# Middle rows of an expert transposed within the next expert's up products, gathers issued earlier in the program, combine weights of all tokens made together

## The chip, the cores and the metric

The kernel runs on one core of a Trainium2 chip. Its engines are named as the profile names them: PE (TensorE, the matrix products), DVE (VectorE), ACT (ScalarE), POOL (GpSimd) and SP (SyncE, which here only issues transfers). Each works through its own queue of instructions in the order in which the program was laid out, and waits at the head of the queue for data or for a buffer. The metric is the device time of one execution in microseconds (us); lower is better.

## The reference

One layer over 512 tokens of width 1024, in float32. Three token mixers (a gated delta rule and two linear attentions with decays) share one input projection, are gated, summed and projected; the result goes through a layer norm. Then comes the part that the change touches, a mixture of 16 experts with a hidden width of 256, of which each token uses two:

```
scores = sigmoid(t @ w_router)
... (one group of four experts is picked, then the top 2 in it: e_idx)
w_sel = take_along_axis(scores, e_idx); w_sel = w_sel / sum(w_sel)
combine = sum(one_hot(e_idx, 16) * w_sel)
h = silu(t @ w_gate[e]) * (t @ w_up[e])
y = sum over e of (h * combine[e]) @ w_down[e]
```

A last layer norm over `alpha*h + y` gives the output.

## The kernel before

The mixers fill the time up to about 635 us, layer norm and routing the time to about 690 us, the experts that to about 853 us, and the rest is the last layer norm and the stores.

A product in float32 is made of three products of rounded halves. `split` (L315) makes them: ACT copies a tile into a rounded high part (CAST, L321), DVE subtracts it from the tile to get the low part (L322). `mm3` (L333) then issues high times high, high times low, low times high (PE, L337 to L339). For weights the high and low parts live in rings of five buffers each (rr_75, 76, 77 and fr_5760, 5761 hold high parts, rr_78, 79, 80 and fr_5762, 5763 low parts), so a cast waits until PE has used the tile five before.

The rows of a token group are handled by slots: each expert has 128 slots. `slots` (L1485) builds one-hot matrices on DVE (L1496) and small products on PE (L1498, L1510) that give, per slot, the token to gather (gidx), the place to scatter to (sidx) and its combine weight (wsl). It does so for four experts at a time, in two experts of the steady part, called slot experts below. For each expert e then:

- `fetch` (L1593) issues its weight transfers on SP (`weights`, six tiles: four of gate and up, two of down), gathers its token rows xg from memory by an indirect transfer on POOL (L1526) into one of three buffers, and transposes xg in `ex_in` (L1536): eight 128x128 transposes on PE (L1541), whose result is split by ACT (L1533) and DVE (L1534) into the tiles xT.
- `ex_up` (L1545) makes the gate and up products: four units u = 0 to 3, each one split weight tile and 6 products, 24 in all.
- `ex_down` (L1560) makes the hidden row (silu on ACT L1562, times up and combine weight on DVE L1563), transposes it (two transposes on PE, L1566), splits the transposed row into the tile mh (ACT CAST L1569, DVE subtraction L1570), then makes 12 down products in two units, copies them out (ACT, L1578) and scatters them (POOL, L1579).

The loop over experts (L1635) calls `ex_up(e)`, then `ex_down(e-1)`, then `fetch(e+1)`, and hooks can insert work behind a unit of `ex_up`. This is the program's order. Each engine's queue is laid out from it by a scheduler that may move instructions of different tiles past each other, when the kernel is built. In the result each PE period holds 24 up products of one expert, two transposes of the row before, eight transposes of the row after, and 12 down products. In this document h0 to h15 are the pairs of row transposes L1566 of experts 0 to 15.

The routing (`choose`, L1315) finds the mask Mb of the chosen experts for two token tiles at a time and hands back `weigh` (L1361), eight small DVE operations (L1364 to L1371) that normalise the scores and put the combine weights, cut in three bf16 pieces, into rc. For tiles 0 and 1 they are called while the first layer norm of tiles 2 and 3 still runs, for tiles 2 and 3 in `slots23`. Instructions of this phase that are pinned to a written order are shown as line L149.

Of the kernel before, what the change touches and what calls it, by code (L numbers as in the profile page):

```python
# [20 lines left out]
T = 512  # L21
# [17 lines left out]
def kernel(  # L39
# [85 lines left out]
    def scr():  # L125
        return scrp.tile([P, T], F32, name="scr", tag="scr", bufs=4)
# [9 lines left out]
    def flat(a):  # L136
        return a.rearrange("p a b -> p (a b)")
# [1004 lines left out]
    E = 16  # L1142
# [174 lines left out]
    def choose(n0, n1, V):  # L1317
# [42 lines left out]

        def weigh():  # L1361

            w = rt[:, 5]
            V.tensor_mul(w, sc, mk)  # L1364
            V.tensor_reduce(um[:, 2], w, axis=mybir.AxisListType.X, op=ALU.add)
            V.reciprocal(um[:, 3], um[:, 2])
            V.tensor_mul(w, w, um[:, 3][:, :, None].to_broadcast([P, m, E]))
            V.tensor_copy(rc[:, n0:n1, :, 3], w)
            V.tensor_sub(w, w, rc[:, n0:n1, :, 3])
            V.tensor_copy(rc[:, n0:n1, :, 4], w)  # L1370
            V.tensor_sub(rc[:, n0:n1, :, 5], w, rc[:, n0:n1, :, 4])  # L1371
# [57 lines left out]
    for n in range(NT):  # L1429
        ps = pst(pp)  # L1430

        between = [lns[i][1](c) for i, c in (((0, 0), (1, 0)), ((0, 1), (2, 0)), ((1, 1), (3, 0)), ((2, 1),))[n] for _ in range(1)]
        steps = [g for g in between for _ in range(2)]
        for u in range(4):
            last = wo_mm(n, u, ws[u], ps)
            if u < len(steps):
                next(steps[u])
            if u == (0 if n == NT - 1 else 2) and n:
                lns[n - 1][4]()
            if u == 2 and n:  # L1440
                lns[n - 1][2]()
            if u == (0 if n == NT - 1 else 2) and n:
                lns[n - 1][3]()
            if u == 2 and n == 2:
                choose(0, 2, V)()
            if u == 2 and n == 3:
                ranks(0, 2, V)
            if u == 3 and n < 2:
                ready.append(split(first[0][n], *(new((P, 2, T), F32R, at="fr") for _ in range(2)), pinned=True))
        lns[n][0](1, ps)  # L1450
# [8 lines left out]
        pass  # L1459
    scores()  # L1460
    rows()
    weigh = choose(2, 4, W)
    ranks(2, 4, W)
    rows0(1, 1, 2)
    drop(*x4)
# [59 lines left out]
    def gather(dst, idx):  # L1525
        return nc.gpsimd.indirect_dma_start(  # L1526
            out=dst, out_offset=None, in_=h1d, in_offset=bass.IndirectOffsetOnAxis(ap=idx, axis=0),
            bounds_check=T - 1, oob_is_err=False)
# [28 lines left out]
                hook[u]()  # L1557
        return ps

    def ex_down(ps, raw, wcol, sidx_col, m=2 * T, e=0):  # L1560
        sg = scr()
        S.activation(sg[:, 0:256], ps[:, 0:256], AF.Silu)  # L1562
        V.scalar_tensor_tensor(sg[:, 256:], ps[:, 256:], wcol, sg[:, 0:256], op0=ALU.mult, op1=ALU.mult)  # L1563
        ps = pst(pm)
        for c in range(2):
            TE.transpose(ps[:, c * P:(c + 1) * P], sg[:, 256 + c * P:256 + (c + 1) * P], ident)  # L1566
        mh = scrp.tile([P, 2, 2, P], F32R, name="mh", tag="scr", bufs=4)
        hT_ = [mh[:, 0], mh[:, 1]]
        S.copy(flat(hT_[0]), ps[:, :256])  # L1569
        sub = V.tensor_sub(flat(hT_[1]), ps[:, :256], flat(hT_[0]).bitcast(F32))  # L1570
        yo = yos((P, D))
        ps = [pst(pp), pst(pp)]
        for k in range(2):
            w = split(raw[4 + k], V=G if e == E - 1 and k == 1 else V)
            for c in range(2):
                mm3(ps[c], lambda b, k: hT_[b][:, k], lambda b, k: w[b][:, c], k, k + 1, k == 0, k == 1)
        for c in range(2):
            S.copy(yo[:, c * T:(c + 1) * T], ps[c])  # L1578
        s = nc.gpsimd.indirect_dma_start(  # L1579
            out=y2d[:m], out_offset=bass.IndirectOffsetOnAxis(ap=sidx_col, axis=0), in_=yo, in_offset=None,  # L1580
            bounds_check=m - 1, oob_is_err=False)
        for o in scats:
            tc.declare_no_dep(s.ins, o.ins, reason="rows of other slots")
        scats.append(s)
        return sub
# [7 lines left out]
    def fetch(e):  # L1593
        wts = weights(e) if e > 1 else first[e]
        if e % 4 == 1 and 1 < e < E - 4:
            slots_of(e + 3, e + 7)()
        xg = xgs[e % 3]
        if e > 1:
            gather(xg, gidx[:, e:e + 1])
        return wts, ex_in(xg)  # L1600


    first.append(weights(1))
# [18 lines left out]

    def slots23():
        rest.append(slots_of(2, 4, W))
        weigh()

    def weights03():
        with tc.issue_after(lows.ins):
# [1 line left out]
        for f in rest:  # L1630
            f()

    hooks = [{2: slots23}, {1: weights03}, {1: lambda: slots_of(4, 8)()}] + [{}] * (E - 3)
    late = None
    for e in range(E):  # L1635
        if e == E - 1:
            ex_down(*late, e=e - 1)
        TE = TP if e == 0 else nc.tensor
        ps = ex_up(xT, wts, ready if e == 0 else (), e, hooks[e])
        if 0 < e < E - 1:  # L1640
            ex_down(*late)
        late = ps, wts, wsl[:, e:e + 1], sidx[:, e:e + 1]
        if e < E - 1:
            wts, xT = fetch(e + 1)
        TE = nc.tensor

    def at_end(src):
# [139 lines left out]
```

## Time and profile before

| | us |
|---|---|
| time, three runs | 887.18, 889.05, 890.28 (median 889.05) |
| the profiled execution | 887.7, its span 885.9 |
| PE busy | 825.9 (93% of the span) |
| DVE busy | 597.9 (67%) |
| ACT busy | 442.0 (50%) |
| POOL busy | 170.9 (19%) |
| mean granted clock of PE | 0.978 of full speed |

The shares are means over stages with different limits, so they don't tell what a change in the expert stage is worth; that is read from the waits and timelines of that stage. PE's records overlap one another (a product of 0.39 us is followed by the next 0.23 us after its start), so the start times tell its pace.

### The profile page before, as it was taken

To read this page: it belongs to the slowest core of one execution; us is meant where nothing else is said; L and a number is where in the kernel's file an instruction comes from. 1 tells how busy PE (TensorE), PEld (TensorE's weight loads), DVE (VectorE), ACT (ScalarE), POOL (GpSimd) and SP (SyncE) were. 2 spreads that over 40 slices of the span, in tenths; PEclk is the share of its full clock that TensorE was granted. 3 is DMA by queue.
4 is the path that set the end of the run, shared out by engine and by line. 5 is a ranking of instruction groups with operands and counts; after the bars stand their busy time and mean duration, and the time that the engine had idled before them with its cause. 6 is when DMAs were issued, how large, how long until landed. Compare 5 with 4: busy or idle time off the path is not lost. (4 is left out here: it accounts for less than half of the span.)

```text
span 885.9 us, 15191 instructions
## 1 busy us (share of the span) xinstructions
PE 825.9 (93%) x5860; PEld 693.5 (78%) x5860; DVE 597.9 (67%) x1104; ACT 442.0 (50%) x824; POOL 170.9 (19%) x197
## 2 busy tenths in 40 slices
PE   8989999999989999999999999999999899999940
PEld 5867878978887999988888888888777678777730
DVE  7775567787675655685934345445477999999838
ACT  6533456645466344475333233234223788888823
POOL 2550001440461330200000000000022132121132
PEclk9989999999999999999999999999999999999985
DMA  6512222022013221234534334336526999999143
GB/s 196 128 56 84 73 72 72 26 72 74 26 72 119 73 72 49 73 120 137 172 96 143 95 95 123 96 105 210 184 79 197 358 357 354 348 367 360 51 160 144
DMA packets 99999, 125.90 MB, mean 142 GB/s; under 512 B 12967, under 2 KB 86775, under 8 KB 99924
## 3 DMA queue, kind: packets, MB, share of 16 engines
q1 hardware_dynamic: 89344, 109.17, 38.4%
q10 hardware_dynamic: 6116, 7.48, 2.6%
q0 software_dynamic: 4464, 8.25, 2.5%
q8 instruction: 47, 0.77, 0.4%
q14 instruction: 28, 0.23, 0.1%
HBM read 118.21 MB, written 14.68 MB: 150 GB/s over the span
## 5 line engine op out<-in xcount | busy, mean ns | idle before, releaser
L322 DVE TENSOR_TENSOR rr<-ff,rr 128x1024 fp32r<-128x1024 f32 x125 | 154.6, 1244 | 112.8 <-ACT rr L321 111.5
L321 ACT CAST rr<-ff 128x1024 fp32r<-128x1024 f32 x126 | 132.1, 1053 | 164.7 <-PE ps L338 126.2
L337 PE MATMUL ps<-rh,rr 128*128 128x512 f32 x384 | 153.7, 400 | 0.0
L338 PE MATMUL ps<-rh,rr 128*128 128x512 f32 x384 | 150.8, 393 | 0.0
L339 PE MATMUL ps<-rh,rr 128*128 128x512 f32 x384 | 150.6, 392 | 0.0
L337 PE MATMUL ps<-rr,rh 128*128 128x256 f32 (+1 forms) x320 | 93.3, 292 | 0.6 <-DVE rh L149 0.6
L339 PE MATMUL ps<-rr,rh 128*128 128x256 f32 (+1 forms) x320 | 91.8, 288 | 0.9 <-issue 0.9
L338 PE MATMUL ps<-rr,rh 128*128 128x256 f32 (+1 forms) x320 | 91.3, 286 | 0.0
L337 PEld LDWEIGHTS ps<-rh,rr 128*128 128x128 f32 x384 | 72.6, 189 | 15.5 <-issue 0.8
L339 PEld LDWEIGHTS ps<-rh,rr 128*128 128x128 f32 x384 | 72.5, 189 | 15.3
L338 PEld LDWEIGHTS ps<-rh,rr 128*128 128x128 f32 x384 | 72.7, 189 | 14.1
L337 PEld LDWEIGHTS ps<-rr,rh 128*128 128x128 f32 x320 | 61.0, 191 | 2.6 <-issue 1.3
L339 PEld LDWEIGHTS ps<-rr,rh 128*128 128x128 f32 x320 | 60.9, 191 | 1.4 <-issue 0.8
L338 PEld LDWEIGHTS ps<-rr,rh 128*128 128x128 f32 x320 | 61.1, 191 | 0.2
L1244 POOL TENSOR_TENSOR ff<-ff,ff 128x512 f32<-128x512 f32 x2 | 2.6, 1278 | 231.7 <-DVE ff L149 231.7
L339 PE MATMUL ps<-ro,rr 128*128 128x512 f32 x96 | 37.4, 389 | 0.0
L337 PE MATMUL ps<-ro,rr 128*128 128x512 f32 x96 | 37.3, 389 | 0.0
L338 PE MATMUL ps<-ro,rr 128*128 128x512 f32 x96 | 37.3, 389 | 0.0
L322 DVE TENSOR_TENSOR fr<-ff,fr 128x1024 fp32r<-128x1024 f32 x30 | 36.1, 1218 | 1.4 <-ACT fr L321 1.3
L321 ACT CAST fr<-ff 128x1024 fp32r<-128x1024 f32 x31 | 32.1, 1054 | 6.2 <-PE ps L339 4.6
L439 DVE SCALAR_TENSOR_TENSOR scr<-ps,vcol,scr 128x511 f32<-128x511 f32 (+2 forms) x36 | 26.6, 742 | 10.7 <-ACT scr L436 10.1
L1579 POOL DMA_INDIRECT y2d<-fl,sidx x16 | 20.3, 1271 | 69.0 <-ACT fl L1578 32.5
(594 smaller groups left out, 1778.5 us busy)
## 6 DMA issues: line engine op xcount, KB each, us to landing
ff<-in_w_in_dram SPq DMA_DIRECT2D x66, 512.0 KB
ff<-in_w_down_dram SPq DMA_DIRECT2D x26, 512.0 KB
ff<-in_w_gate_dram SPq DMA_DIRECT2D x48, 256.0 KB
ff<-in_w_up_dram SPq DMA_DIRECT2D x48, 256.0 KB
ff<-in_w_out_dram SPq DMA_DIRECT2D x8, 512.0 KB
ff<-y2d SPq DMA_DIRECT2D x6, 512.0 KB
fh<-in_w_gate_dram SPq DMA_DIRECT2D x11, 256.0 KB
fh<-in_w_up_dram SPq DMA_DIRECT2D x11, 256.0 KB
```

Of the source, the lines that this page charges most:

```text
L321: S.copy(a, src)
L322: i = V.tensor_sub(b, src, a.bitcast(F32))
L337: TE.matmul(ps, w(0, k), h(0, k), start=start and k == k0, stop=False)
L338: TE.matmul(ps, w(0, k), h(1, k), start=False, stop=False)
L339: last = TE.matmul(ps, w(1, k), h(0, k), start=False, stop=stop and k == k1 - 1)
L439: V.scalar_tensor_tensor(y[:, sh:], ps[:, :T - sh], convw[:, j, j0:j0 + 1], y[:, sh:], op0=ALU.mult, op1=ALU.add)
L1244: act[0] = G.tensor_mul(xg3[:, cs], t[:, cs], g1r[:, cs])
L1579: s = nc.gpsimd.indirect_dma_start(out=y2d[:m], out_offset=bass.IndirectOffsetOnAxis(ap=sidx_col, axis=0), in_=yo, in_offset=None, bounds_ ...
```

## The change

Three edits. The hidden part of `ex_down` becomes a function of its own, `ex_hidden`; for experts e = 2 to 14 the one of expert e-1 is now called by the hook behind unit 2 of `ex_up(e)`, between the third and the fourth unit, and `ex_down(e-1)` gets its result. `fetch(e+1)` now stands ahead of `ex_down(e-1)` in the program, and inside `fetch(e)` the gather is that of expert e+1. Third, both calls of `weigh` are made in `slots23`, and the tile w of each is one of its own. The first expert and the last two keep their order.

```
 
         def weigh():
 
-            w = rt[:, 5]
+            w = scr()[:, :m * E].rearrange("p (m e) -> p m e", e=E)
             V.tensor_mul(w, sc, mk)
             V.tensor_reduce(um[:, 2], w, axis=mybir.AxisListType.X, op=ALU.add)
             V.reciprocal(um[:, 3], um[:, 2])
...
             if u == (0 if n == NT - 1 else 2) and n:
                 lns[n - 1][3]()
             if u == 2 and n == 2:
-                choose(0, 2, V)()
+                weighs = [choose(0, 2, V)]
             if u == 2 and n == 3:
                 ranks(0, 2, V)
             if u == 3 and n < 2:
...
         pass
     scores()
     rows()
-    weigh = choose(2, 4, W)
+    weighs.append(choose(2, 4, W))
     ranks(2, 4, W)
     rows0(1, 1, 2)
     drop(*x4)
...
                 hook[u]()
         return ps
 
-    def ex_down(ps, raw, wcol, sidx_col, m=2 * T, e=0):
+    def ex_hidden(ps, wcol):
         sg = scr()
         S.activation(sg[:, 0:256], ps[:, 0:256], AF.Silu)
         V.scalar_tensor_tensor(sg[:, 256:], ps[:, 256:], wcol, sg[:, 0:256], op0=ALU.mult, op1=ALU.mult)
...
         hT_ = [mh[:, 0], mh[:, 1]]
         S.copy(flat(hT_[0]), ps[:, :256])
         sub = V.tensor_sub(flat(hT_[1]), ps[:, :256], flat(hT_[0]).bitcast(F32))
+        return hT_, sub
+
+    def ex_down(ps, raw, wcol, sidx_col, m=2 * T, e=0, hidden=None):
+        hT_, sub = hidden or ex_hidden(ps, wcol)
         yo = yos((P, D))
         ps = [pst(pp), pst(pp)]
         for k in range(2):
...
         wts = weights(e) if e > 1 else first[e]
         if e % 4 == 1 and 1 < e < E - 4:
             slots_of(e + 3, e + 7)()
-        xg = xgs[e % 3]
-        if e > 1:
-            gather(xg, gidx[:, e:e + 1])
-        return wts, ex_in(xg)
+        if e < E - 1:
+            gather(xgs[(e + 1) % 3], gidx[:, e + 1:e + 2])
+        return wts, ex_in(xgs[e % 3])
 
 
     first.append(weights(1))
...
 
     def slots23():
         rest.append(slots_of(2, 4, W))
-        weigh()
+        for f in weighs:
+            f()
 
     def weights03():
         with tc.issue_after(lows.ins):
...
         for f in rest:
             f()
 
-    hooks = [{2: slots23}, {1: weights03}, {1: lambda: slots_of(4, 8)()}] + [{}] * (E - 3)
+    hooks = [{2: slots23}, {1: weights03}, {1: lambda: slots_of(4, 8)()}] + [{} for _ in range(E - 3)]
     late = None
     for e in range(E):
         if e == E - 1:
             ex_down(*late, e=e - 1)
         TE = TP if e == 0 else nc.tensor
+        hid = []
+        if 1 < e < E - 1:
+            hooks[e][2] = lambda: hid.append(ex_hidden(late[0], late[2]))
         ps = ex_up(xT, wts, ready if e == 0 else (), e, hooks[e])
-        if 0 < e < E - 1:
-            ex_down(*late)
+        done = late
         late = ps, wts, wsl[:, e:e + 1], sidx[:, e:e + 1]
         if e < E - 1:
             wts, xT = fetch(e + 1)
+        if 0 < e < E - 1:
+            ex_down(*done, hidden=hid[0] if hid else None)
         TE = nc.tensor
 
     def at_end(src):
```

Place one, the row transposes h6 of expert 6, around the end of the up products of expert 7. PE before (ro tiles are xT, rr and fr tiles are weights, mh is the split row):

```order
L337 MATMUL ps<-rr_76,ro_4206 128x512
L338 MATMUL ps<-rr_79,ro_4206 128x512
L339 MATMUL ps<-rr_76,ro_4208 128x512
L1566 MATMUL ps<-ident,scr 128x128 x2
L1541 MATMUL ps<-ident,fl_6360 128x128 x8
L337 MATMUL ps<-rr_77,mh 128x512
```

PE in the changed kernel:

```order
L339 MATMUL ps<-rr_75,ro_4208 128x512
L1566 MATMUL ps<-ident,scr 128x128 x2
L337 MATMUL ps<-rr_76,ro_4206 128x512
L338 MATMUL ps<-rr_79,ro_4206 128x512
L339 MATMUL ps<-rr_76,ro_4208 128x512
L337 MATMUL ps<-rr_76,ro_4206 128x512
L338 MATMUL ps<-rr_79,ro_4206 128x512
L339 MATMUL ps<-rr_76,ro_4208 128x512
L1541 MATMUL ps<-ident,fl_6352 128x128 x8
L337 MATMUL ps<-rr_77,mh 128x512
```

The two transposes L1566 moved ahead of the last six up products, and the eight of L1541 now stand alone ahead of the down products.

ACT at the same place, before:

```order
L321 CAST fr_5761<-ff_94 128x1024
L321 CAST rr_75<-ff_86 128x1024
L321 CAST rr_76<-ff_90 128x1024
L1569 CAST mh<-ps 128x256
L1533 CAST ro_4205<-ps 128x512 x2
L1562 ACTIVATE scr<-ps 128x256
```

ACT in the changed kernel:

```order
L321 CAST fr_5760<-ff_102 128x1024
L321 CAST fr_5761<-ff_94 128x1024
L321 CAST rr_75<-ff_86 128x1024
L1569 CAST mh<-ps 128x256
L321 CAST rr_76<-ff_90 128x1024
L1533 CAST ro_4205<-ps 128x512 x2
L1562 ACTIVATE scr<-ps 128x256
```

The copy into mh moved ahead of one cast of a weight tile; one cast (rr_75) still stands ahead of it.

Place two, DVE around the same row, before:

```order
L322 TENSOR_TENSOR fr_5762<-ff_102,fr_5760 128x1024
L322 TENSOR_TENSOR fr_5763<-ff_94,fr_5761 128x1024
L322 TENSOR_TENSOR rr_78<-ff_86,rr_75 128x1024
L1496 TENSOR_TENSOR fl_6357<-slot,pos 128x512
L1570 TENSOR_TENSOR mh<-ps,mh 128x256
L1534 TENSOR_TENSOR ro_4207<-ps,ro_4205 128x512 x2
L322 TENSOR_TENSOR rr_79<-ff_90,rr_76 128x1024
```

DVE in the changed kernel:

```order
L322 TENSOR_TENSOR rr_80<-ff_100,rr_77 128x1024
L322 TENSOR_TENSOR fr_5762<-ff_102,fr_5760 128x1024
L1570 TENSOR_TENSOR mh<-ps,mh 128x256
L322 TENSOR_TENSOR fr_5763<-ff_94,fr_5761 128x1024
L322 TENSOR_TENSOR rr_78<-ff_86,rr_75 128x1024
L1534 TENSOR_TENSOR ro_4207<-ps,ro_4205 128x512 x2
L322 TENSOR_TENSOR rr_79<-ff_90,rr_76 128x1024
```

The subtraction for mh moved ahead of two splits of the next expert's weights (into fr_5763 and rr_78).

Place three, DVE in the routing, where the addition L149 into ff_84 is what PE next waits for. Before (L1383 and L1384 belong to the slots of the first tiles, the rs chain is a reciprocal root of the layer norm):

```order
L1383 TENSOR_TENSOR pos<-pos,ps 128x32
L1371 TENSOR_TENSOR rc<-scr,rc 128x32
L193 TENSOR_SCALAR rs_6201<-rs_6201 128x1
L1384 TENSOR_TENSOR ff_86<-slot,pos 128x256
L197 SCALAR_TENSOR_TENSOR rs1o<-rs_6201 128x1
L1285 TENSOR_TENSOR mv_5801<-mv_5801,rs1o 128x1
L1308 SCALAR_TENSOR_TENSOR ff_103<-ff_103,rs1o,ff_100 128x1024
L1275 SCALAR_TENSOR_TENSOR lg<-gb,mv_5801 128x16
L149 TENSOR_TENSOR ff_84<-ff_84,ps 128x512
```

DVE in the changed kernel:

```order
L1383 TENSOR_TENSOR pos<-pos,ps 128x32
L197 SCALAR_TENSOR_TENSOR rs1o<-rs_6193 128x1
L1384 TENSOR_TENSOR ff_86<-slot,pos 128x256
L1285 TENSOR_TENSOR mv_5801<-mv_5801,rs1o 128x1
L1308 SCALAR_TENSOR_TENSOR ff_103<-ff_103,rs1o,ff_100 128x1024
L1275 SCALAR_TENSOR_TENSOR lg<-gb,mv_5801 128x16
L149 TENSOR_TENSOR ff_84<-ff_84,ps 128x512
```

The combine-weight operation L1371 is gone from this place, as are seven others ahead of it; they stand later, among the pinned operations of the second `choose`, and those of the second `weigh` stand behind them.

## Rows read from the trace of the kernel before

**Rows 1.** Windows: busy us (instructions) per engine, clock, DMA share, GB/s

```profile
740.00:760.00 20.00, 19.32 (x94) 15.75 (x94) 19.20 (x23) 17.21 (x25) 5.90 (x5) 1.00 1.02 364
...
820.00:850.00 30.00, 27.09 (x130) 21.20 (x128) 22.23 (x27) 22.00 (x33) 8.90 (x6) 1.00 0.13 44
```

**Rows 2.** Waits of TensorE: what it waited for, us in total, times, longest

```profile
PE ps L337 <- ACT mh L1569: 4.7, 13, 0.8
...
PE ps L1566 <- DVE scr L1563: 1.9, 2, 1.0
...
PE ps L149 <- DVE ff L149: 1.6, 1, 1.6
```

**Rows 3.** Timeline of PE: start us, us, line, operation, [idle before <-releaser]

```profile
753.22 0.38 PE L1566 MATMUL ps<-ident,scr 128*128 128x128 f32 x2
...
753.43 1.04 PE L1541 MATMUL ps<-ident,fl 128*128 128x128 f32 x8
...
754.79 0.50 PE L337 MATMUL ps<-rr,mh 128*128 128x512 f32 x1 [0.32 <-ACT mh L1569]
...
762.89 0.39 PE L339 MATMUL ps<-rr,ro 128*128 128x512 f32 x1
...
763.12 0.38 PE L1566 MATMUL ps<-ident,scr 128*128 128x128 f32 x2
```

**Rows 4.** Timeline of ACT at the same place

```profile
753.42 1.05 ACT L321 CAST rr<-ff 128x1024 fp32r<-128x1024 f32 x1 [0.27 <-DMA ff<-in_w_gate_dram]
...
754.37 0.36 ACT L1569 CAST mh<-ps 128x256 fp32r<-128x256 f32 x1
...
754.63 1.08 ACT L1533 CAST ro<-ps 128x512 fp32r<-128x512 f32 x2
```

**Rows 5.** Timeline of PE: four transposes alone between products

```profile
737.30 0.60 PE L1541 MATMUL ps<-ident,fl 128*128 128x128 f32 x4
...
737.66 0.48 PE L337 MATMUL ps<-rr,ro 128*128 128x512 f32 x1
...
737.97 0.40 PE L338 MATMUL ps<-rr,ro 128*128 128x512 f32 x1
```

**Rows 6.** Timeline of DVE in the same expert

```profile
752.30 2.35 DVE L322 TENSOR_TENSOR fr<-ff,fr 128x1024 fp32r<-128x1024 f32 x2
...
754.77 0.42 DVE L1570 TENSOR_TENSOR mh<-ps,mh 128x256 fp32r<-128x256 f32 x1
...
755.25 1.29 DVE L1534 TENSOR_TENSOR ro<-ps,ro 128x512 fp32r<-128x512 f32 x2
...
758.73 0.48 DVE L1563 SCALAR_TENSOR_TENSOR scr<-ps,wsl,scr 128x256 f32<-128x256 f32 x1
```

**Rows 7.** Timeline of PE in a slot expert, to the next pair

```profile
773.07 0.38 PE L1566 MATMUL ps<-ident,scr 128*128 128x128 f32 x2
...
774.64 0.50 PE L337 MATMUL ps<-fr,mh 128*128 128x512 f32 x1
...
783.47 0.38 PE L1566 MATMUL ps<-ident,scr 128*128 128x128 f32 x2
```

**Rows 8.** Timeline of DVE beside it: one-hots

```profile
771.66 1.89 DVE L1496 TENSOR_TENSOR fl<-slot,pos 128x512 bf16<-128x512 f32 x3
```

**Rows 9.** Timeline of SP: the last weight tile issued

```profile
807.39 0.37 SPq L1404 DMA_DIRECT2D ff<-in_w_up_dram  x1
```

**Rows 10.** Timeline of ACT: the last weight tile cast

```profile
843.82 1.06 ACT L321 CAST fr<-ff 128x1024 fp32r<-128x1024 f32 x1
```

**Rows 11.** Timeline of DVE in the routing

```profile
667.65 0.26 DVE L1371 TENSOR_TENSOR rc<-scr,rc 128x32 bf16<-128x32 f32 x1
...
669.88 0.68 DVE L149 TENSOR_TENSOR ff<-ff,ps 128x512 f32<-128x512 f32 x1
```

**Rows 12.** Timeline of PE beside it

```profile
670.61 0.66 PE L149 MATMUL ps<-ident,ff 128*128 128x128 f32 x4 [1.62 <-DVE ff L149]
```

**Rows 13.** Timeline of POOL: a gather in the steady part

```profile
744.77 1.52 POOL L1526 DMA_INDIRECT fl<-h1d,gidx  x1 [3.42 <-PE ps L1541]
```

More of the change, by code (lines that the diff above doesn't have):

```diff
@@ L1361, in weigh @@
         def weigh():
-            w = rt[:, 5]
+            w = scr()[:, :m * E].rearrange("p (m e) -> p m e", e=E)
             V.tensor_mul(w, sc, mk)
@@ L1444 @@
             if u == 2 and n == 2:
-                choose(0, 2, V)()
+                weighs = [choose(0, 2, V)]
             if u == 2 and n == 3:
@@ L1461 @@
     rows()
-    weigh = choose(2, 4, W)
+    weighs.append(choose(2, 4, W))
     ranks(2, 4, W)
@@ L1558, in ex_up, with ex_hidden @@
         return ps
-    def ex_down(ps, raw, wcol, sidx_col, m=2 * T, e=0):
+    def ex_hidden(ps, wcol):
         sg = scr()
@@ L1570, in ex_down @@
         sub = V.tensor_sub(flat(hT_[1]), ps[:, :256], flat(hT_[0]).bitcast(F32))
+        return hT_, sub
+    def ex_down(ps, raw, wcol, sidx_col, m=2 * T, e=0, hidden=None):
+        hT_, sub = hidden or ex_hidden(ps, wcol)
         yo = yos((P, D))
@@ L1596, in fetch @@
             slots_of(e + 3, e + 7)()
[L1597 to L1600, printed above, removed]
+        if e < E - 1:
+            gather(xgs[(e + 1) % 3], gidx[:, e + 1:e + 2])
+        return wts, ex_in(xgs[e % 3])
     first.append(weights(1))
@@ L1624, in slots23 @@
         rest.append(slots_of(2, 4, W))
-        weigh()
+        for f in weighs:
+            f()
     def weights03():
@@ L1631, in weights03 @@
             f()
-    hooks = [{2: slots23}, {1: weights03}, {1: lambda: slots_of(4, 8)()}] + [{}] * (E - 3)
+    hooks = [{2: slots23}, {1: weights03}, {1: lambda: slots_of(4, 8)()}] + [{} for _ in range(E - 3)]
     late = None
@@ L1638 @@
         TE = TP if e == 0 else nc.tensor
+        hid = []
+        if 1 < e < E - 1:
+            hooks[e][2] = lambda: hid.append(ex_hidden(late[0], late[2]))
         ps = ex_up(xT, wts, ready if e == 0 else (), e, hooks[e])
-        if 0 < e < E - 1:
-            ex_down(*late)
+        done = late
         late = ps, wts, wsl[:, e:e + 1], sidx[:, e:e + 1]
@@ L1644 @@
             wts, xT = fetch(e + 1)
+        if 0 < e < E - 1:
+            ex_down(*done, hidden=hid[0] if hid else None)
         TE = nc.tensor
```

## The prediction

> **What bounds the kernel now.** I read the windows first, because the page's shares are means over unlike stages. In the steady part of the experts PE is busy 19.3 of 20 us, DVE 19.2 and ACT 17.2, the 16 DMA engines are full, and the clock is granted in full [rows 1]. Four resources are near their end, so the next view has to say which ends last. The waits of PE do: in the expert stage its largest entry is the first down product waiting for ACT's copy into mh, 13 times, 4.7 us; waits for weight splits or weight transfers do not appear among its entries [rows 2]. The reader is to see that PE sets the pace and loses a little at one place per expert.
>
> The timelines show how. The row transposes of an expert begin at 753.22, the eight transposes at 753.43, and the first down product only at 754.79 [rows 3]. On ACT a weight cast begins at 753.42, as PE releases a buffer, and the copy into mh, ready to run since the two transposes ended, stands behind it until 754.37 [rows 4]. The first product starts when that copy is done (754.73). The period, from one pair of row transposes to the next, is 763.12 - 753.22 = 9.90 us [rows 3].
>
> **The hidden part moved (first term).** How long does PE really stand? Four transposes alone take 0.36 us until the next product starts (737.30 to 737.66), and their record lasts 0.60; eight have a record of 1.04, so each further one takes 0.11 and eight take 0.36 + 4 x 0.11 = 0.80 [rows 3, 5]. Before, PE was free at 753.43 + 0.80 = 754.23 and stood until 754.79: 0.56 us. The record says 0.32, since it counts from the modelled end of the last transpose; that is the lower end. I take 0.50, near to what the starts give. Thirteen rows, h1 to h13, are hoisted. Two of them (the slot experts) had no wait, and two of the 13 waits belong to h14 and h15, which are not hoisted: 11 waits go, 11 x 0.50 = 5.5 us (3.5 to 6.2).
>
> The pair now stands alone amid products, and PE changes from products to transposes once more. After four transposes the next product took 0.31 (737.66 to 737.97) where the pace is 0.23 (762.89 to 763.12) [rows 3, 5]: 0.08 to 0.09 more, 13 times, 1.1 us. Net -4.4 (-2.4 to -5.1).
>
> Is mh in time at its new place? From the start of the pair PE has 0.21 for the pair, 0.09 for the change, 6 x 0.23 = 1.38 for the last unit and 0.80 for the eight transposes: the first down product can start at 2.48. ACT's queue still has one cast ahead of the copy, released as now; by [rows 4] the copy ends 754.73 - 753.22 = 1.51 after the pair starts. The reserve is 0.97 us. The low part follows on DVE, 0.4 later [rows 6], and is wanted a product later.
>
> What is queued behind: on DVE the subtraction for mh now stands ahead of two splits that it used to follow, so DVE may wait there for PE and ACT. Its work in a plain expert is six splits at 2.35 a pair, 1.29, 0.42 and 0.48 [rows 6]: 7.05 + 2.19 = 9.24 us, less some 0.5 by which neighbouring records overlap, in a new period of 9.90 - 0.41 = 9.49. It fits, with 0.25 to 0.75 to spare. In a slot expert four one-hots at 0.63 [rows 8] add 2.5. Before, such an expert's hand-over (773.07 to 774.64) shows no wait, since small slot products of PE filled the time, and its period was 783.47 - 773.07 = 10.40 [rows 7]. After, work of 11.2 to 11.7 stands against 10.5, the lead that a ring of five tiles allows shrinks, and I expect 0 to 0.4 late at a split behind each of two slot experts: +0.3 in all (0 to 0.8). Behind it, plain experts catch up.
>
> The Trainium skill, TensorE: Matmul & The Clock Gate, Part 4: PE-mode transpose, gives about 275 ns for a transpose in a kernel's context. By an estimate from that figure a pair alone among products would take 0.55 in place of 0.21, 13 x 0.34 = 4.4 us more, and this term would come out at nothing. The trace differs for transposes in a row: 0.11 apiece beyond the first four [rows 3, 5].
>
> **The fetch moved.** Issuing the gather of e+1 in fetch(e), and the fetch ahead of the down part, leaves the queues of POOL and SP as they were but for buffer names. POOL already gathers right behind the transposes that free its buffer [rows 13], which is what three experts ahead with three buffers allows. Casting the weights sooner needs them landed sooner: the last tile is issued at 807.39 [rows 9], DMA falls to a share of 0.13 after 820 [rows 1], and the last casts begin at 843.82 [rows 10]. A PE that is 5 us earlier eats about a fifth of those 24 us. Cost 0 (-0.3 to +0.5).
>
> **The combine weights together.** Before the addition for which PE waits 1.62 us [rows 12], eight operations of `weigh` went; the last stands at 667.65, in the chain that leads to the addition at 669.88 [rows 11]. What they hold up there is the two or three that can't fall into a gap, at some 0.1 each: -0.3 (0 to -0.6). At their new place the eight sit between dependent operations of a chain that waits for each result, and the second eight move out of the crowded start of the expert stage. I count 0 for that (-0.2 to +0.4).
>
> **The first experts.** The same reordering lets expert 0's hidden row be made before two splits of expert 2; PE waited 1.9 us in two places for such rows [rows 2]; one of them is h0. The pair h1 and what follows then come earlier by up to the 1.9, less what the splits put back lose. I take a third, -0.6 (+0.5 to -1.5).
>
> **Sum.** -4.4 + 0.3 + 0 - 0.3 - 0.6 = -5.0. The end of the kernel hangs on the last scatter behind the last down product, so it moves with PE. Profiled execution: 887.7 - 5.0 = 882.7. That execution lies 1.35 under the median of the runs, 889.05; from the median the sum gives 884.05, and I forecast 884.0. With the ends of the terms the likeliest case spans 881.0 to 886.5.
>
> **Rivals.**
> - DVE becomes the bound. For: 19.2 of 20 us busy. Its mean need over a plain trio and a slot expert is 9.24 + 2.5/4 = 9.87, against a mean PE period of 10.03 before (three of 9.90, one of 10.40 [rows 3, 7]). Then the eight periods up to 800 gain 0.16 each, the four after them, without one-hots, 0.41 each, the routing 0.3, and half of the early term stays: 1.3 + 1.6 + 0.3 + 0.3 = 3.5 at best; I take 2.7, with one more wait of 0.4 in each slot expert, 886.4. Against: the overlap of records makes the need smaller, and DVE's present idle time is a wait for casts, not for PE's results. 0.14.
> - The copy is late all the same. ACT reaches it more than 0.97 us later than now, because the cast ahead of it waits for something else, or casts run late. The wait moves and the extra change of PE's work is paid: with the routing's 0.3 and half of the early term, 889.05 + 1.1 - 0.6 = 889.5. Against: ACT is 86% busy and the cast ahead is released by the product just before the pair. 0.09.
> - Transfers set the pace. For: a share of 1.02 and 364 GB/s [rows 1]. If weights could come no sooner, nothing is gained before 800 and only the last four hoisted rows (4 x 0.41) and the routing pay: 887.1. The Trainium skill, Perfetto Trace Analysis, Engine Utilization (Roofline), puts the per-core share of memory bandwidth at 358 GB/s and allows a lone core some 120% of that; by the first figure the steady part is at its limit, by the second it has a fifth left. The trace bears out only that the engines are full, for the lead of 20 us and more says that PE does not wait for them. 0.04.
> - Slower. DVE stands at the head of its queue for mh. If it arrives as early as the ring lets it, it idles until the copy is done, 1.5 after the pair starts, and the two splits behind it start late. From an idle of 0.5 per period it eats the reserve, from 0.9 on the period is longer than before; at 1.4 it is 8.95 + 1.4 = 10.35, 0.45 more than 9.90, 13 times: 889.05 + 5.9 = 895. Against: a DVE that is behind doesn't arrive early, so this wait limits itself. 0.05.
> - More than forecast, by the first experts' gain at its far end and the full 0.56: about 881. 0.04.
>
> **Chances.** The forecast has 0.64. About 0.3% (2.7 us) is what a measurement of this kernel can tell from no change, so faster means under 886.4. Nearly all of the forecast (0.62), two thirds of the DVE rival (0.09), the last case (0.04) and a rest give 0.76; within 0.3%: 0.18; slower 0.06. The range for 8 in 10 reaches over the DVE and transfer rivals to 887.4.
>
> **What would show it.** Right: the wait of the first down product for mh falls from 13 times to two or three, the period of plain experts from 9.90 to about 9.5, DVE's share in the steady part rises, and the wait for the addition in the routing shrinks from 1.62 to about 1.3. Wrong: waits of PE for splits (L322) or for xT (L1534) appear among its entries; the waits for mh stay; DVE idles ahead of L1570 for more than 0.5 per expert; or casts wait for transfers.

## The result and the profile after

The changed kernel takes 882.99 us (median of 9 runs, 880.54 to 886.54) beside 888.99 us of the kernel before (9 runs, 886.90 to 890.28): a ratio of 0.9944, 95% interval 0.9924 to 0.9963, 6.0 us faster. The forecast was 884.0, 5.0 us faster.

The profiled execution of the changed kernel has a span of 882.6 us, 3.3 less than that of before. It is a little slower than the median of its nine runs (884.35 us beside 882.99); a second profile of the same kernel, made with the experiments, has a span of 878.5. The difference of these two lies ahead of the first row transposes and in the tail; the expert stage is the same in both to a few hundredths.

First PE's waits (what it waited for, us in total, times, longest), to be set beside [rows 2]. One entry of the kernel before that [rows 2] doesn't show:

```profile
PE ps L149 <- DMA fl<-h1d,gidx: 1.1, 1, 1.1
```

The waits of the changed kernel:

```profile
PE ps L149 <- DMA fl<-h1d,gidx: 3.3, 1, 3.3
...
PE ps L337 <- ACT mh L1569: 1.4, 3, 0.8
...
PE ps L149 <- DVE ff L149: 1.3, 1, 1.3
...
PE ps L1566 <- DVE scr L1563: 1.0, 1, 1.0
...
PE ps L1498 <- DVE fl L1496: 0.7, 1, 0.7
```

The wait for mh went from 13 times to 3 (h0, h14, h15), as forecast, and no wait for a weight split or an expert's xT takes its place in the steady part. The largest entry is now the wait for the first gather, 3.31 us where it was 1.05; this was not forecast.

Then the timeline of PE in one expert, to be set beside [rows 3] (start us, us, line, operation):

```profile
752.04 0.38 PE L1566 MATMUL ps<-ident,scr 128*128 128x128 f32 x2
...
752.18 0.48 PE L337 MATMUL ps<-rr,ro 128*128 128x512 f32 x1
...
752.49 0.39 PE L338 MATMUL ps<-rr,ro 128*128 128x512 f32 x1
...
753.65 1.03 PE L1541 MATMUL ps<-ident,fl 128*128 128x128 f32 x8
...
754.44 0.48 PE L337 MATMUL ps<-rr,mh 128*128 128x512 f32 x1
...
761.40 0.38 PE L1566 MATMUL ps<-ident,scr 128*128 128x128 f32 x2
```

The reader is to see three distances. From the eight transposes to the first down product it is 754.44 - 753.65 = 0.79 us, where it was 1.36: 0.57 less, and no wait is noted. From the pair to the next product it is 0.14, and that product is followed after 0.31 instead of 0.23. From one pair to the next it is 761.40 - 752.04 = 9.36 instead of 9.90.

ACT at the same place (beside [rows 4]):

```profile
752.29 1.05 ACT L321 CAST fr<-ff 128x1024 fp32r<-128x1024 f32 x1 [0.31 <-DVE rr L322]
...
753.25 0.36 ACT L1569 CAST mh<-ps 128x256 fp32r<-128x256 f32 x1
...
753.85 1.05 ACT L321 CAST rr<-ff 128x1024 fp32r<-128x1024 f32 x1 [0.24 <-PE ps L339]
```

The copy into mh still stands behind a cast, as the order said, and begins 1.21 us after the pair (1.15 before). But it ends at 753.61, before PE has begun the eight transposes. The cast is still in the way; nobody waits for it any more.

DVE there (beside [rows 6]):

```profile
753.64 0.42 DVE L1570 TENSOR_TENSOR mh<-ps,mh 128x256 fp32r<-128x256 f32 x1 [0.22 <-ACT mh L1569]
...
753.98 1.22 DVE L322 TENSOR_TENSOR fr<-ff,fr 128x1024 fp32r<-128x1024 f32 x1
```

The subtraction for mh waits 0.22 us for the copy at the head of DVE's queue; from 715 to 815 us DVE's waits hold this five times, 1.1 us in all. The wait that the slower rival built on is there, at a sixth of the 1.4 us at which that rival was priced.

Windows (busy us per engine with instructions, clock, DMA share, GB/s), first of the kernel before:

```profile
690.00:700.00 10.00, 7.61 (x52) 5.47 (x52) 8.55 (x23) 6.78 (x9) 2.27 (x2) 1.00 1.00 357
```

Then of the changed kernel, the second line beside [rows 1]:

```profile
690.00:700.00 10.00, 6.46 (x34) 5.05 (x35) 4.65 (x11) 3.76 (x6) 2.27 (x2) 0.66 0.80 291
...
740.00:760.00 20.00, 20.00 (x99) 16.61 (x98) 19.56 (x23) 18.41 (x26) 7.22 (x5) 1.00 0.98 347
```

PE is now busy all of the steady stretch and DVE 19.56 of 20 us. In the first ten us after the routing the granted clock is 0.66 of full speed (a mean of the two levels, 1.2 and 2.4 GHz), after PE had stood idle for 3.31 us; before, with an idle time of 1.05, it was 1.00 there.

### The profile page after: what moved, and what is told of

Read it like the earlier page. It is cut to its first block, busy times and chain, and to the rows that moved or that the text cites. A ratio compares the mean times of both kernels' runs of the same rounds, so it can differ in the third digit from the quotient of the medians.

```text
span 882.6 us, 15196 instructions
## 1 busy us (share of the span) xinstructions
PE 823.4 (93%) x5860; PEld 692.9 (79%) x5860; DVE 596.8 (68%) x1104; ACT 442.5 (50%) x824; POOL 176.0 (20%) x197
## 4 chain that ended last, share of the span: by engine, by line
PE 74%; DVE 10%; issue 5%; DMA 4%; ACT 4%; POOL 2%; DVEq 0%; SPq 0%; POOLq 0%; ACTq 0%
PE ps L337 19%; PE ps L339 19%; PE ps L338 19%; PE ps L149 5%; PE ps L911 1%; PE ps L1541 1%; DVE rr L322 1%; DMA y2d<-fl,sidx 1%; DMA ff<-y2d 1%; PE ps L939 1%; PE ps L656 1%; PE ps L941 1%; DMA fl<-h1d,gidx 1%; PE ps L898 1%; DVE ff L149 1%
## 5 line engine op out<-in xcount | busy, mean ns | idle before, releaser
L1583 POOL DMA_INDIRECT y2d<-fl,sidx x16 | 27.6, 1727 | 64.1 <-ACT fl L1582 49.7
```

Of the source, the lines that this page charges most:

```text
L1583: s = nc.gpsimd.indirect_dma_start(out=y2d[:m], out_offset=bass.IndirectOffsetOnAxis(ap=sidx_col, axis=0), in_=yo, in_offset=None, bounds_ ...
```

## The experiments

Every variant is laid out anew by the scheduler, so the order of each queue has to be read again before a difference is put down to the edit. In several experiments below, the copy put first and the loaded DVE above all, it moved more than the edit did.

**Undo the place alone.** The changed kernel, with the hidden part called one unit later:

```
-            hooks[e][2] = lambda: hid.append(ex_hidden(late[0], late[2]))
+            hooks[e][3] = lambda: hid.append(ex_hidden(late[0], late[2]))
```

> The changed kernel with the hidden part called behind the fourth unit of the up products instead of the third, all else as changed. Theory A: the pair of transposes stands directly ahead of the eight again, ACT's copy behind a cast, 11 waits for mh return, plain periods 9.9, time 888.5. Rival B (the place does not matter, the new program order does): 883 and periods of 9.35.

Measured: ratio to the kernel before 0.9987 (0.9973 to 1.0002), median 887.91; plain periods 9.91 to 10.00. PE and then ACT in one expert:

```profile
754.00 0.38 PE L1566 MATMUL ps<-ident,scr 128*128 128x128 f32 x2
...
754.21 1.04 PE L1541 MATMUL ps<-ident,fl 128*128 128x128 f32 x8
...
755.57 0.50 PE L337 MATMUL ps<-rr,mh 128*128 128x512 f32 x1 [0.32 <-ACT mh L1569]
```

```profile
754.20 1.05 ACT L321 CAST rr<-ff 128x1024 fp32r<-128x1024 f32 x1 [0.27 <-DMA fh<-in_w_up_dram]
...
755.15 0.37 ACT L1569 CAST mh<-ps 128x256 fp32r<-128x256 f32 x1
```

The three rows of PE are those of [rows 3] again: pair, eight, 0.32 of recorded wait. The new functions and the new program order alone bring nothing that can be told from no change; the place among the up products does it.

**Remove the cause without the change.** The kernel before, where the casts of the third unit of experts 3 to 14 may not be queued ahead of the copy:

```
-        S.copy(flat(hT_[0]), ps[:, :256])
+        cop[0] = S.copy(flat(hT_[0]), ps[:, :256])
...
+            elif u == 2 and 2 < e < E - 1:
+                with tc.issue_after(cop[0].ins):
+                    w = split(raw[u])
```

> The kernel before, with one thing changed: in experts 3 to 14 the cast of the third up unit's weights may not pass ACT's copy into mh, so that the copy runs as soon as the row transposes are done. No part of the change is in it. Theory A (the wait is made by that cast in ACT's queue, not by the distance between the transposes and the down products): the wait of the first down product falls from 0.56 to about 0.3 or less, plain periods 9.5 to 9.7, time 885 to 887. Rival B (the distance is what counts: the copy itself needs the time): periods 9.9, time 889.

Measured: ratio 0.9977 (0.9960 to 0.9994), median 886.76; plain periods 9.62 to 9.71. PE and ACT:

```profile
754.21 0.38 PE L1571 MATMUL ps<-ident,scr 128*128 128x128 f32 x2
...
754.43 0.60 PE L1541 MATMUL ps<-ident,fl 128*128 128x128 f32 x4
...
755.05 0.50 PE L337 MATMUL ps<-rr,mh 128*128 128x512 f32 x1
...
756.10 0.38 PE L1541 MATMUL ps<-ident,fl 128*128 128x128 f32 x2
...
758.18 0.38 PE L1541 MATMUL ps<-ident,fl 128*128 128x128 f32 x2
```

```profile
754.63 0.37 ACT L1574 CAST mh<-ps 128x256 fp32r<-128x256 f32 x1 [0.52 <-PE ps L1571]
...
754.90 1.05 ACT L321 CAST rr<-ff 128x1024 fp32r<-128x1024 f32 x1
```

The copy now runs right behind the transposes and the cast behind it. The first product comes 0.62 us after the transposes instead of 1.36, although only four of the eight transposes stand in between: four would take 0.36, so some 0.26 of wait is left, the time of the copy itself. The mean plain period falls from 9.95 to 9.66, and with the change it is 9.35: 0.29 for the queue and 0.30 more with the distance, half and half.

But the layout moved, too. The other four transposes now stand amid and behind the down products (756.10 and 758.18), so the distance that the kernel before had is halved. With all eight in between PE would not have been free before 754.43 + 0.80 = 755.23, after the copy's end at 755.00. By that estimate the whole wait of the kernel before comes from the cast ahead of the copy, and the 0.26 left here, the time that the copy itself takes, from the four transposes that are gone from in between. No run has the copy first and all eight behind the pair, so this is not shown.

**Each edit alone.** The hoist alone, with fetch, gather and combine weights as before:

```
+        if 1 < e < E - 1:
+            hooks[e][2] = lambda: hid.append(ex_hidden(late[0], late[2]))
         ps = ex_up(xT, wts, ready if e == 0 else (), e, hooks[e])
...
+            ex_down(*late, hidden=hid[0] if hid else None)
         late = ps, wts, wsl[:, e:e + 1], sidx[:, e:e + 1]
```

> Only the hoist of the hidden part; fetch, gather and combine weights as before. Theory A (the gain is the wait of the first down product for mh, and the fetch ahead of the down part is needed so that the eight transposes fill the place between the last up unit and the down products): without it the transposes come behind the down products, close ahead of the up products that need them; the waits for mh vanish, waits for xT come, periods are uneven between 9.4 and 10.5, time 885 to 891. Rival B (the hoist carries the whole gain alone): plain periods 9.35, time 883.5.

Measured: ratio 0.9964 (0.9949 to 0.9980), median 885.35. The waits for mh are gone (two left, those of h14 and h15), but the expected waits for xT did not appear in the list. The order in which PE's instructions were laid out is irregular: the pair sometimes stands in the up products and sometimes amid the eight transposes, and those are cut into two or three groups. Over eleven periods (from expert 2's silu to expert 13's) it takes 108.1 us, where the kernel before takes 110.3 and the changed one 105.0. In the expert stage the hoist alone gives two fifths of what it gives with the fetch ahead; by the times it is between a half and two thirds. How the rest is lost (more groups, each with its slow first product, and short waits) was not taken apart.

The fetch and the gather alone, the hidden part behind the up products:

```
         late = ps, wts, wsl[:, e:e + 1], sidx[:, e:e + 1]
         if e < E - 1:
             wts, xT = fetch(e + 1)
+        if 0 < e < E - 1:
+            ex_down(*done, hidden=hid[0] if hid else None)
...
```

(No hook fills `hid` here.)

> Only the fetch ahead of the down part with the gather of the next expert; the hidden part stays behind the up products. Theory A: 11 or more waits for mh of 0.3 or more by the record stay, plain periods 9.9, time 889 (887.5 to 891). Rival B (the order of the fetch is what pays): time 885 or less and fewer waits.

Measured: ratio 1.0044 (1.0026 to 1.0063), median 892.57: slower, and above the range expected. Its waits of PE:

```profile
PE ps L337 <- ACT mh L1569: 6.8, 13, 1.2
...
PE ps L1541 <- DMA fl<-h1d,gidx: 2.4, 1, 2.4
```

The waits for mh grow from 4.7 to 6.8, and the second gather is late once, by 2.39 us. The loss is at the front: the first three periods are 11.44, 13.50 and 11.50 us, those from the fourth on mostly 9.9 to 10.0 as before. Putting the fetch ahead does not help by itself; it is the hoist's other half, since it lets the eight transposes stand between the up and the down products in every expert.

The combine weights alone:

```
-                choose(0, 2, V)()
+                weighs = [choose(0, 2, V)]
...
-        weigh()
+        for f in weighs:
+            f()
...
```

> Only the combine weights together. Theory A: the wait for the addition in the routing falls from 1.62 to about 1.25 us, and this is taken back by the wait for the first gather, which hangs on the store of the last token rows; the periods stay 9.9 and the time 888.5, within noise of before. Rival B (the early part brings two or three us): 886.

Measured: ratio 1.0014 (0.9996 to 1.0032), median 889.82: no change. Its waits of PE:

```profile
PE ps L149 <- DMA fl<-h1d,gidx: 2.0, 1, 2.0
...
PE ps L149 <- DVE ff L149: 1.3, 1, 1.3
```

The wait for the addition falls from 1.62 to 1.25, and the wait for the first gather rises from 1.05 to 2.00. That rise can't be put down to the edit alone: in this profile the clock was granted in full from 680 to 685 us, where it was 0.75 in the kernel before, and the profiles further down show longer waits for the gather whenever that is so. The other way round, the changed kernel without this edit:

```
-                weighs = [choose(0, 2, V)]
+                choose(0, 2, V)()
...
```

> The changed kernel with the combine weights made as before: the hoist and the fetch ahead together, without the third edit. Theory A (these two carry all of the gain, and the fetch ahead pays only together with the hoist): plain periods 9.35, the wait for the addition in the routing 1.6 again, ratio 0.993 to 0.996. Rival B (the third edit carries part of it): 0.9965 or more.

Measured: ratio 0.9937 (0.9917 to 0.9956), median 882.40, beside 0.9936 (0.9916 to 0.9955) for the changed kernel on the same chip. The third edit is worth nothing that can be measured.

**A unit earlier.**

```
-            hooks[e][2] = lambda: hid.append(ex_hidden(late[0], late[2]))
+            hooks[e][1] = lambda f=hooks[e].get(1): (f and f(), hid.append(ex_hidden(late[0], late[2])))
```

> The changed kernel with the hidden part called one unit earlier, behind the second unit. Theory A: the copy had 0.9 us in hand already, so another 1.36 us changes nothing: plain periods 9.35, time 883 (882 to 884.5). Rival B (DVE, over 97% busy, stands at the subtraction for mh and pays for the earlier place): DVE waits of more than 0.5 ahead of it, periods 9.5 or more, 885 or more.

Measured: ratio 0.9903 (0.9885 to 0.9920), median 880.32. The plain periods are 9.39, 0.04 longer than with the third unit, so the steady part gains nothing from more distance, as expected. Yet the time is lower than expected. In its profile the wait for the first gather is 0.7 us and the clock stays at 1.00 behind it. But the profiled execution is one of the two slowest of the six (883.06; the other four take 878.47 to 880.49 at a higher mean clock), so the profile doesn't show why those are fast. That made the first gather and the clock around it the open question.

**Load DVE.** The changed kernel with L1563 issued three times:

```
         V.scalar_tensor_tensor(sg[:, 256:], ps[:, 256:], wcol, sg[:, 0:256], op0=ALU.mult, op1=ALU.mult)
+        V.scalar_tensor_tensor(sg[:, 256:], ps[:, 256:], wcol, sg[:, 0:256], op0=ALU.mult, op1=ALU.mult)
+        V.scalar_tensor_tensor(sg[:, 256:], ps[:, 256:], wcol, sg[:, 0:256], op0=ALU.mult, op1=ALU.mult)
```

> The changed kernel with the multiplication L1563 issued three times instead of once (the same values), 0.4 us each: 0.8 us of DVE work more per expert. Theory A (DVE is busy 97 to 98% of the time but has no more than 0.1 to 0.6 us to spare per plain period): DVE becomes the bound, PE waits for splits appear, periods rise by 0.3 to 0.7, time 886 to 891. Rival B (DVE's records overlap and it still has a full us to spare): periods 9.35 to 9.45, time 883 to 884.

Measured: ratio 1.0097 (1.0079 to 1.0116), median 898.06, slower than the upper end expected (891). Its waits of PE:

```profile
PE ps L338 <- DVE fr L322: 1.4, 1, 1.4
...
PE ps L338 <- DVE rr L322: 0.9, 2, 0.7
```

And PE at a plain pair, h9:

```profile
804.41 0.41 PE L1568 MATMUL ps<-ident,scr 128*128 128x128 f32 x2
...
804.66 1.04 PE L1541 MATMUL ps<-ident,fl 128*128 128x128 f32 x8
...
805.72 0.50 PE L337 MATMUL ps<-rr,mh 128*128 128x512 f32 x1
```

The two slot experts take 13.35 us each, about 3 more than with the change alone, and the two long waits for splits (0.74 and 1.39) stand there: in a slot expert 0.8 us more of DVE work is more than DVE has to spare. The plain experts say less than was hoped. From h4 on the pair stands directly ahead of the eight transposes again, so the layout has undone the hoist there, and the periods of 9.66 to 9.97 hold that as well as the load. No wait for a split shows in them. How much DVE had to spare in a plain period is therefore not shown; the two periods ahead of the first slot expert, with the pair still amid the products, are 9.59 and 9.41. The expected range also had no room for the longer wait for the first gather (4.2 us) in that profile.

**The first gather.** The changed kernel with the weight transfers of experts 4 and 5, and so all behind them on SP, held until the first gathered rows have landed:

```
-        wts = weights(e) if e > 1 else first[e]
+        if e in (4, 5):
+            with tc.issue_after(hold.ins):
+                wts = weights(e)
+        else:
+            wts = weights(e) if e > 1 else first[e]
...
     gather(xgs[1], gidx[:, 1:2])
+    hold = nc.sync.dma_start(dr.tile([1, 64], F32, name="hold")[:, 0:64], xgs[1][0:1, 0:64])
```

> The changed kernel, with the weight transfers of experts 4 and later held on SP until the first gathered rows have landed (a transfer of 256 bytes that reads them stands ahead). Theory A (the 3.31 us that PE waits for the first gather come from weight transfers in the same DMA engines, and the fall of the granted clock behind it from that wait): the gather lands by about 689, PE waits under 0.7 us, the clock stays at 1.00 from 690 to 700, h0 is 3 us or more earlier, time 880. Rival B (the store of the last rows sets it): the gather lands no sooner, time 883. Rival C (the weights are then late): waits for weight transfers in the steady part, 885 or more.

Measured: ratio 0.9904 (0.9884 to 0.9923), median 880.38. PE's wait for the first gather:

```profile
PE ps L149 <- DMA fl<-h1d,gidx: 0.2, 1, 0.2
```

The wait is nearly gone, as expected, and the clock is 1.00 from 690 to 700. But the gather is issued only at 686.33 in this profile and first used at 692.93, not by 689, and h0 is 2.0 us earlier (702.33 beside 704.37), not 3.

Then the changed kernel, the hold, and the hold with the earlier hook on one chip:

> The changed kernel itself, beside the next three on the same chip, since its wait for the first gather (3.31 us in its profile, 2.1, 0.7 and 4.2 in three others with the same early program) seems to vary from execution to execution. Theory A: periods 9.35 once more to 0.02, the wait for the first gather anything from 0.7 to 4.2 us, ratio 0.992 to 0.996. Rival B (the wait is the same in every execution of this program): 3.3 us again, with the clock at 0.66 behind it.

> The kernel with held weight transfers, beside the changed kernel on one chip. Theory A (the transfers of later weights delay the first gather): wait for the gather 0.2 to 0.7 us, clock 1.00 from 690 to 700, 2 to 4 us faster than the changed kernel beside it, ratio to the kernel before 0.989 to 0.992. Rival B (chips differ, the hold does nothing on the whole): the two within 0.15%.

> The kernel with held weight transfers, and the hidden part behind the second unit instead of the third. Theory A (the earlier hook changes nothing in the experts; its low time before was a short wait for the gather): equal to the kernel with held transfers within 0.15%, plain periods 9.39 against 9.35. Rival B (the earlier place is worth the 2 to 3 us that it seemed to have over the changed kernel): faster than the kernel with held transfers by 0.2% or more.

Measured: the changed kernel 0.9936 (0.9916 to 0.9955), median 882.28; with the hold 0.9910 (0.9890 to 0.9930), 879.73; with the hold and the earlier hook 0.9893 (0.9872 to 0.9914), 878.84. Where both ran on one chip the hold is 0.26% ahead of the changed kernel, with intervals that overlap; only the last of the three stands clear of it, barely. In the earlier job, where the changed kernel did not run beside it, the hold has the ratio of the earlier hook without a hold (0.9904 and 0.9903). So the hold shortens a wait, as the profiles show, but what it is worth in time is not settled. Nor is it settled whether the earlier hook adds anything to it: the two are 0.10% apart, within what was expected, the plain periods are 9.39 against 9.35, and the profiled execution of the last was one with a full clock through this stretch. The last is the fastest version run.

The profiles say what varies. Windows of the changed kernel's first profile (680 to 685), of its second (680 to 685, 690 to 700), and of the hold with the earlier hook (the same two):

```profile
680.00:685.00 5.00, 5.00 (x44) 4.78 (x44) 4.93 (x14) 1.83 (x3) 0.37 (x1) 1.00 0.96 329
```

```profile
680.00:685.00 5.00, 5.00 (x39) 4.99 (x38) 3.39 (x12) 0.78 (x2) 0.49 (x1) 0.76 0.81 281
...
690.00:700.00 10.00, 8.15 (x55) 6.10 (x55) 8.55 (x19) 7.02 (x9) 2.26 (x2) 1.00 0.99 353
```

```profile
680.00:685.00 5.00, 5.00 (x42) 4.69 (x41) 4.93 (x14) 1.67 (x4) 1.47 (x1) 1.00 0.79 240
...
690.00:700.00 10.00, 8.30 (x65) 6.45 (x62) 9.49 (x19) 7.61 (x12) 2.20 (x2) 1.00 0.92 298
```

In the first profile the stretch from 680 to 685 ran at full clock, PE was early at the transposes of the first gathered rows and stood there 3.31 us; the clock then fell. In the second it ran at 0.76, and PE waited 0.82. So it goes in all eleven profiles without the hold: four had the full clock in that stretch and waits of 2.0 to 4.2 us for the gather, seven had a clock of 0.66 to 0.86 and waits of 0.7 to 1.1. What a full clock gives at 680 is taken back at 690, since the gather does not land sooner. With the hold and a full clock no wait is left, and the first row transposes begin at 698.53. That is a single profile. They began at 704.37 and 701.18 in the two of the changed kernel and at 702.33 and 701.15 in the two of the hold alone, whose clock was 0.66 from 680 to 685.

The rival that named the store of the last token rows (the gather reads what it writes) holds a part. In the loaded-DVE profile the indices were ready at 682.86, that store landed at 684.96, and the gather was issued at 685.88, 0.92 later. In the profiles with a lower clock the indices come last, and the gather follows them after 0.9. So at a full clock early indices don't bring an earlier gather; the weight transfers beside it then lengthen its way.

## Why the prediction was right

**The wait for mh** went, by the mechanism forecast. Its size was on the low side: 0.57 per expert against 0.50, so 11 x 0.57 = 6.3 against 5.5. The recorded 0.32 was indeed too little.

**The change of PE's work** is the term that was mis-sized. The prediction charged 13 times 0.08 to 0.09 (1.1 us) for the slow first product behind a pair that stands alone. That slow product is there (0.31 instead of 0.23), but the pair costs 0.14 to the next product instead of the 0.21 that was kept for it: 0.22 in all, 0.01 more than before. A transpose that is followed by a product is left sooner than one that is followed by a transpose; the 0.21 had been read from a pair followed by transposes. So by these sizes the net of the first term is -6.1, not -4.4.

**The reserve.** The copy ended at 753.61, the first down product began at 754.44: 0.83 us in hand, where 0.97 was forecast. The undone place and the earlier place came out as that reckoning has it.

**The slot experts** were forecast 0.3 worse in all; their periods are 10.23 and 10.55 where they were 10.40 both: 0.0. That is the low end of what was allowed for. With 0.8 us more of DVE work these two became 13.35 with PE waiting for splits, so the margin there is smaller than that.

**The fetch** was forecast to cost nothing, by its queues. That holds only beside the hoist. By itself it makes the kernel slower, and the hoist without it gives about half of the gain. The prediction took the order of the changed program as given and did not ask which edit made it.

**The routing** term (-0.3) came at its place; whether it reaches the end depends on the execution. PE's rows in the changed kernel, beside [rows 12]:

```profile
670.87 0.66 PE L149 MATMUL ps<-ident,ff 128*128 128x128 f32 x4 [1.25 <-DVE ff L149]
```

The wait is 1.25, 0.37 less. But in this profile the next thing that is late, the first gather, does not come sooner, so PE waits for it longer. POOL and PE there:

```profile
684.63 1.29 POOL L1526 DMA_INDIRECT fl<-h1d,gidx  x1 [9.12 <-DVE rr L149]
```

```profile
693.08 1.97 PE L149 MATMUL ps<-ident,fl 128*128 128x128 f32 x8 [3.31 <-DMA fl<-h1d,gidx]
```

The gather is issued at 684.63, as in the kernel before (684.72), though its indices (gidx) were ready 1.3 us earlier, at 682.5; PE has its rows 8.45 us later. In the second profile, whose clock was as low from 680 to 685 as in the kernel before (0.76 and 0.75), the gain does come through: the rows are there at 691.73, 0.45 earlier than the 692.18 of the kernel before. By the times of the two experiments on this edit it is within the noise. The prediction named no wait for this transfer although [rows 2]'s view had it with 1.1 us.

**The first experts** (-0.6): the wait for h0's row went, and one of 0.73 for a one-hot came right behind it. From the pair h0 to the last product it is 143.2 us in both profiles of the changed kernel against 150.0, 6.8 less, of which the 11 waits are 6.3. The wait for h0's row ended where this stretch begins, so its loss is not in the 6.8, and what makes up the rest (0.5, or 0.6 with the 0.01 that each pair now costs more) was not taken apart. Ahead of h0, from the first use of the gathered rows on, the second profile of the changed kernel takes 9.45 us where the kernel before takes 10.18: 0.7 less, near to the 0.6 forecast.

**The sum.** Within the expert stage, from h0 to the last product, it is -6.8 in both profiles, where the forecast had -4.1 for the hoist and the slot experts. The second profile can be set beside that of the kernel before, since the clock fell at the same place in both: -0.45 up to the first gathered rows, -0.7 from there to h0, -6.8 to the last product, +0.55 in the tail behind it, -7.4 in all. The first profile gives back more (its wait for the gather, the clock behind that, 1.5 in the tail); the tail is 33.2 to 36.1 us from the start of the last product over all profiles taken, and why is not known. The nine runs spread over 6 us, and the medians differ by 6.0. So the mechanism was right, and the forecast was short by 2.7 in the expert stage: 1.0 by the change of PE's work, 0.8 by the size of the wait, 0.3 by the slot experts, and 0.6 that was not taken apart. That the median came within 1 us of the forecast is partly luck, for it keeps only 6.0 of the 7.4 that this pair of profiles shows; where the runs without a profile lose the rest is not on record.

That DVE becomes the bound did not come: PE has no wait for a split or an xT from 706 to 830 us, though DVE is 98% busy. The rival in which DVE idles ahead of the subtraction started from a period of 8.95 us that the prediction does not work out; its need of 9.24 less the 0.5 of overlap would be 8.74. The idle time measured, 0.22, is below the 0.5 from which on that rival counted.

Of the rivals, transfers that set the pace are ruled out for the steady part: DMA moved 347 GB/s there at a share of 0.98, periods shortened all the same. The Trainium skill, Perfetto Trace Analysis, Engine Utilization (Roofline), treats some 120% of 358 GB/s as a lone core's ceiling; the steady part moved 343 to 370 GB/s over 20 us in these profiles and PE had no wait for a weight transfer there, so no run here shows where the ceiling is. The Trainium skill's about 275 ns for a transpose (TensorE: Matmul & The Clock Gate, Part 4: PE-mode transpose) is the length of one such record here, 0.27 us, but not its cost: records overlap, and a pair alone took 0.14 us to the next product. The prediction's estimate by that figure, 0.55 for a pair, took the length for the pace.

## What to carry to other kernels

A wait that comes round in every iteration can be made by one long instruction of a shared engine's queue, issued just before the short one that is waited for; moving the producer a step earlier hid both here, and putting the short one first got half of it, in a layout that also took four transposes out from in between. Before charging for a new switch on an engine, read the cost of both ends of the old one. Edits that each do little or harm can need each other: undo each alone before crediting any, and read the order of the queues in each variant, for a build can undo one edit when another is tried. And where the clock or a transfer varies between executions, a gain ahead of a transfer that is late anyway is only handed on to that wait.

## What was not expected of the hardware

The transfers in flight beside it lengthen the way of a small gather: from issue to first use it took 7.2 to 8.5 us in the profiles without the hold, 5.6 to 6.6 with it, in two of these three with no wait of PE at its end. The granted clock was 1.00 and 0.76 at the same place (680 to 685 us) in two executions of the changed kernel, and behind an idle time of PE of 3.3 and 4.2 us it fell in the next ten us to 0.66 and 0.74, but not behind 2.0 and 2.1. DVE ran at 98% busy in the steady part without a single wait of PE for it in the list from 706 to 830 us.
